# A hybrid attention/scan/FFN block on one core: first FFN column pair as eight plain products, and gate pieces of the dense filler moved to the end of the scan

## The chip, the cores and the metric

One Trainium2 chip, one core. The metric is the device time of one launch in microseconds (us); lower is better. The five engines are named as in the profile: PE (TensorE matmuls; PEld is its weight load), DVE (VectorE), ACT (ScalarE), POOL (GpSimd) and SP (SyncE, which here only issues DMAs).

## The reference, cut to what matters

One layer on 1024 tokens of width 1024, all in float32: a norm, one wide projection, three token mixers (two attentions of 8 heads and a state-space scan of 16 heads), a gated merge, then an FFN with a causal convolution.

```
u = rms_norm(x) @ w_in                       # split: mla | fox | ssm (z, xBC, dt) | gate (3 x 1024)
xBC = silu(causal_dwconv(xBC))               # 4 taps; input of the scan
y_a = mla(u_mla) @ w_br_mla;  y_b = fox(u_fox) @ w_br_fox;  y_c = ssd(u_ssm) @ w_br_ssm
g = sigmoid(u_gate + b_gate)
x = x + (g0 * y_a + g1 * y_b + g2 * y_c) @ w_out
a = causal_dwconv(rms_norm(x) @ w_up)        # w_up: 1024 x 5632; 3 taps
gate, val = split(a, 2)                      # 2816 columns each
x = x + (silu(gate) * val) @ w_down
```

## The kernel before, in words

Every large product is made of three float32r matmuls (high by high, high by low, low by high part). An operand is therefore "split": ACT copies it rounded into a high tile (line 142 in `split`), DVE subtracts to get the low tile (line 143). A matmul moves 512 columns through a 128x128 weight block.

**The dense filler.** 36 column blocks of 128 columns of `u` (12 of xBC, called conv blocks, and 24 gate blocks, `g_d`) are not computed in a stage of their own. The generator `all_fill` produces them in pieces of six matmuls (line 794, target `mm`); after each piece it yields 1.3 (us, the planner's price of a piece). A block has two halves of 24 matmuls, so 8 pieces; there are 288 pieces, 1728 matmuls. Before a block's matmuls its weights are loaded by SP (`wr`, 512 KB, line 741) and split on ACT and DVE (lines 744, 745). Behind each half ACT reads PSUM: a plain copy for conv blocks (line 799 and 801), a tanh for gate blocks. A conv block then runs its taps on POOL, DVE and ACT and is stored to `xbc_d`; a gate block is stored to `g_d` by SP (line 808). The list `blocks` sets the order of the blocks.

**Who pulls the filler.** `merge(streams, fill_us)` interleaves the streams of one step (for attention: scores of one unit, values of the unit two before; for the scan: parts a, b, c of chunks c, c-1, c-2) with `fill_us` worth of filler. In attention, 64 units plus two, it is `FILL_ATT` times the planner's cost of the unit's own PE work (which adds up to 231.7 over all units); in the scan's ten steps it is `FILL_SSD[c]`. Before attention 8.0 are taken, before the scan 10.0. Within attention and scan the PE order is the planner's; the other engines are placed by the scheduler. What is left of the filler after the scan is drained before the branch products start.

**End of the scan.** For the last chunk, part b ends with a multiplication by z (line 1153), a square with row sum on ACT (line 1156) into the single `yT` buffer, a reciprocal square root on DVE, and a scaling on ACT (line 1161); part c transposes the result on PE (`stp`, line 1169), ACT copies it to `yT` (line 1170) and SP stores it (`ys_d`, line 1172). Then the branch products follow (`ybr`, line 167 in `mm3`), in the order fox, mla, ssm. Each first loads its input (`ar`, through four buffers `t4` that the filler's gate tiles and z tiles also use), splits it (`ah`, `al`), and multiplies.

**The FFN's up projection.** It runs over 22 column pairs i (gate columns i and value columns i + 22). Rows are in two halves of 512 tokens, the contraction in two halves of 512 features; `B11`, `B21`, `T1`, `B22` are the four blocks or sums of the normed activations. A pair is computed by a Strassen-Winograd scheme in seven block products of 12 matmuls (`product`, line 1319) in place of eight: `ua` two (against B11 and B21), `ub`, `uc` twice, `ud` twice. The scheme needs sums of weights (`sums`, on POOL: S12 and S34, lines 1409 to 1413), which are then split, and sums of activations `T3`, `T2`, `T4`, made once: the buffer `T3f` is split into the high and low tiles `cbh` and `cbl` (`t_split`, lines 1442 and 1445), then changed in place (`t_sums`, lines 1452 to 1456, two of four rows on DVE, two on POOL), and split again. The `ua` products of the first four pairs are taken early, right behind the output projection `wo`, and kept in `cg`. Each pair ends with the convolution (lines 1515 to 1523) on ACT and DVE. The raw weights of a pair sit in two `wr` buffers, so the next pair's loads wait for this pair's sums and for the split of a third piece (`h22`).

All PE work from `wo` on stands in written order (`order2`).

Of the kernel before, what the change touches and what calls it, by code (L numbers as in the profile page):

```python
# [11 lines left out]
F32 = mybir.dt.float32  # L12
# [3 lines left out]
AF = mybir.ActivationFunctionType  # L16
ALU = mybir.AluOpType
# [4 lines left out]
P = 128  # L22
# [15 lines left out]
def f32(ap):  # L38
    return ap.bitcast(F32)
# [3 lines left out]
def block_kernel(ctx: ExitStack, tc: tile.TileContext, x, positions, norm_mix_g, w_in, b_gate,  # L43
# [91 lines left out]
    def uid(s):  # L135
        cnt[0] += 1
        return f"{s}_{cnt[0]}"
# [639 lines left out]
    def all_fill():  # L777

        conv = [("c", j, C_XBC + j * P) for j in range(12)]
        gates = [(b, j, C_G + b * D + j * P) for b in (1, 0, 2) for j in range(NK)]  # L780
        blocks = [e for n in range(12) for e in (conv[n], gates[n])] + gates[12:]
        nxt = fill_load(blocks[0][2])
        for n, (kind, j, c0) in enumerate(blocks):
            wh, wl, rl = nxt
            if n + 1 < len(blocks):
                nxt = fill_load(blocks[n + 1][2])
            force(rl[0])
            u, ul = f_t4.get()
            for half in range(2):
                ps, pl = f_ps.get()  # L790
                hs = slice(512 * half, 512 * half + 512)
                for k in range(NK):
                    for i, (a, b) in enumerate(((wh, hnh), (wh, hnl), (wl, hnh))):
                        T.matmul(ps, a[:, k, :], b[half][:, k, :], start=(k == 0 and i == 0),  # L794
                                 stop=(k == NK - 1 and i == 2))
                    if k % 2 == 1 and k < NK - 1:
                        yield 1.3
                if kind == "c":
                    fn = lambda ps=ps, hs=hs, u=u: A.activation(u[:, hs], ps, AF.Copy)
                else:  # L800
                    fn = lambda ps=ps, hs=hs, u=u, r=8 * kind + j: A.activation(
                        u[:, hs], ps, AF.Tanh, bias=pc_g[:, r:r + 1], scale=0.5)
                pl[0] = later(1.4, fn)
                if half == 1:
                    if kind == "c":
                        conv_done(j, u, ul, 2.2)
                    else:
                        ul[0] = later(2.0, lambda u=u, g=g_d[kind][j]: SY.dma_start(g, u))
                yield 1.3
# [172 lines left out]
    def cost_v(jp):  # L982
        return 0.88 * jp + 0.33 + 0.39

    FILL_ATT = 1.08
    FILL_SSD = [12.0] * 8 + [12.0, 8.0]
    with ExitStack() as pt__:
        atp = pt__.enter_context(TP("atp", 2))
        psp = pt__.enter_context(TP("psa", 1, space=PSUM))
# [332 lines left out]
    def bank(name):  # L1322
        return psp.tile([P, 512], F32, name=uid(name), tag="up", bufs=6)
# [28 lines left out]
    xrp = po_.enter_context(TP("x2p", 1))  # L1352
    gff = bcast(norm_ffn_g[0], D, "gff", xrp)
    x2r = [None] * NT
    first = []
    units = [(t, nh) for nh in range(2) for t in range(3)] + [(t, nh) for t in range(3, NT) for nh in range(2)]

    head = [psp.tile([P, 512], F32, name=uid("wo"), tag="up", bufs=6) for _ in range(3)]
# [9 lines left out]
    for t, nh in units:  # L1368
        ns = slice(512 * nh, 512 * nh + 512)
        if nh == 0 and 4 <= t < 4 + FIRST:  # L1370
            n = t - 4
            if n == 0:
                r0 = raws(pairs[0])
                raw = r0[0]
            else:
                raw = fpl.tile([P, NK, P], F32, name=uid("wr"), tag="t4", bufs=4)
                SY.dma_start(raw, upv[:, :, pairs[n] * P:pairs[n] * P + P])
            first.append(halves(raw) if n < 3 else raw)
# [18 lines left out]
    a_ = []  # L1397
    for n in range(3):
        a_.append(bank("ua"))
        product(a_[n], first[n], 0, *B11)  # L1400
    norm2(NT - 1, x2r[NT - 1])
    po_.close()

# [9 lines left out]
        G.tensor_sub(S34[:, 4:8, :], ri[:, 4:8, :], S12[:, 4:8, :])  # L1413
        return S12, S34

    S_ = sums(*r0)
    h22_ = halves(r0[1][:, 4:8, :], 4)
    done_ = []
    for n in range(3):
        c_ = upb.tile([P, S], F32, name=uid("cg"), tag="cg", bufs=FIRST)  # L1420
        A.activation(c_[:, 512:], a_[n], AF.Copy)
        done_.append(c_)
    for n in range(FIRST):
        if n == 3:
            first[n] = halves(first[n])
            a_.append(bank("ua"))
            product(a_[n], first[n], 0, *B11)
            done_.append(upb.tile([P, S], F32, name=uid("cg"), tag="cg", bufs=FIRST))
            A.activation(done_[n][:, 512:], a_[n], AF.Copy)
        product(a_[n], first[n], 4, *B21, first=False)  # L1430
        A.activation(done_[n][:, 0:512], a_[n], AF.Copy)
    cbp = pcb.enter_context(TP("cb", 1))
    cbh = cbp.tile([P, 12, 512], F32R, name="cbh", tag="cbh")
    cbl = cbp.tile([P, 12, 512], F32R, name="cbl", tag="cbl")
# [12 lines left out]
    def t_sums(second):  # L1447

        for k in range(4):
            e = G if k > 1 else V  # L1450
            if second:
                e.tensor_add(tf[k], tf[k], f32(B11[0][k]))
                e.tensor_add(tf[k], tf[k], f32(B11[1][k]))
            else:
                e.tensor_sub(tf[k], f32(B21[0][k]), tf[k])
                e.tensor_add(tf[k], tf[k], f32(B21[1][k]))

    def tmp(name, bufs=1):
        return upa.tile([P, 512], F32, name=uid(name), tag=name, bufs=bufs)

    for n, i in enumerate(pairs):
        early = n < FIRST
        ri, rj = r0 if n == 0 else raws(i)
# [9 lines left out]
        S12, S34 = S_ if n == 0 else sums(ri, rj)  # L1473
        hS12 = halves(S12)
        hS34 = halves(S34)
        h22 = h22_ if n == 0 else halves(rj[:, 4:8, :], 4)
        if n > 0:
# [7 lines left out]
        if n == 0:  # L1485
            t_split(T3)
        product(d0, hS34, 0, *T3)
        e5 = tmp("e5")
        A.activation(e5, c0_, AF.Copy)
        if n == 0:  # L1490
            t_sums(True)
            t_split(T2)
        e7 = tmp("e7")
        A.activation(e7, d0, AF.Copy)
        product(c0_, hS34, 4, *B22, first=False)
        if n == 0:
            t_sums(False)
            t_split(T4)
# [12 lines left out]
        V.tensor_add(cv[:, 0:512], d0, X)  # L1511
        av = []
        for j, c in ((i, cg), (i + NFF, cv)):
            a = fpl.tile([P, S], F32, name=uid("fa"), tag="t4", bufs=4)
            A.activation(a, c, AF.Identity, bias=pc_f2[:, 44 + j:45 + j], scale=pc_f2[:, j:j + 1])
            for d in (1, 2):
                w = pc_f1[:, 44 * (2 - d) + j:44 * (2 - d) + j + 1]
                V.scalar_tensor_tensor(out=a[:, d:], in0=c[:, :S - d], scalar=w, in1=a[:, d:],
                                       op0=ALU.mult, op1=ALU.add)
            av.append(a)  # L1520
        A.activation(av[0], av[0], AF.Silu)
        V.tensor_mul(av[1], av[0], av[1])
        SY.dma_start(act_d[i], av[1])

    wd = ffn_w_down[0].rearrange("(r p) c -> r p c", p=P)
# [150 lines left out]
```

## Time and profile before

| what | value |
|---|---|
| time, median of 3 runs | 2149.49 us (2144.91 to 2150.79) |
| time of the profiled execution | 2144.91 us |
| its span, first to last instruction | 2143.0 us |
| mean granted PE clock | 0.982 of full speed |
| busy: PE, DVE, ACT, POOL | 2042.3, 1402.9, 936.0, 649.0 us |
| filler matmuls (line 794) | 1728, in three groups of 576 |

The span is the time of the profiled execution less 1.9 us around it. That execution is the fastest of the three. Attention lies at about 436 to 973 us of the span, the scan at 973 to 1193, the branch products at 1207 to 1384, the output projection at 1384 to 1478, the up projection from 1478 to about 1935, and the down projection behind it.

### The profile page before, as it was taken

How to read it: one execution, taken by the hardware profiler on the slowest of the kernel's cores; microseconds unless marked ns; L12 is line 12 of the kernel's file. 1: busy time of each engine (PE TensorE's matmuls, PEld its weight loads, DVE VectorE, ACT ScalarE, POOL GpSimd, SP SyncE). 2: the span in 40 equal slices, each digit the busy share in tenths (PEclk: the TensorE clock that was granted, in tenths of full speed). 3: DMA queues.
4: the chain of work that ended last, by engine and by line, in shares of the span. 5: the costliest groups of instructions: out<-in, count | busy, mean ns of one | idle time of the engine just before them, and what ended most of it. 6: DMA issues, size and time to landing. Idle time of an engine off the chain costs nothing.

```text
span 2143.0 us, 29100 instructions
## 1 busy us (share of the span) xinstructions
PE 2042.3 (95%) x10253; PEld 1689.7 (79%) x10253; DVE 1402.9 (65%) x2590; ACT 936.0 (44%) x1677; POOL 649.0 (30%) x620
## 2 busy tenths in 40 slices
PE   7999898999999999999999799999889999999999
PEld 6898677778888787787777688888668888887887
DVE  6687477346666566665888446557976677665665
ACT  5554222145555555554555213223444454545432
POOL 2453132212222222220000021002655544441855
PEclk9999999999999999999999899999899999999999
DMA  5167668654343544524342556441122222229765
GB/s 169 33 190 222 220 216 240 205 156 126 96 137 97 138 121 109 131 86 127 105 134 89 162 184 204 140 134 61 49 86 82 88 79 80 88 74 338 260 217 190
DMA packets 276649, 303.61 MB, mean 142 GB/s; under 512 B 19308, under 2 KB 209784, under 8 KB 276504
## 3 DMA queue, kind: packets, MB, share of 16 engines
q1 hardware_dynamic: 276504, 301.76, 46.0%
q8 instruction: 81, 1.33, 0.3%
q14 instruction: 64, 0.52, 0.1%
HBM read 209.03 MB, written 92.67 MB: 141 GB/s over the span
## 4 chain that ended last, share of the span: by engine, by line
PE 78%; DVE 7%; DMA 5%; POOL 3%; ACT 3%; issue 3%; SPq 0%; DVEq 0%; ACTq 0%; POOLq 0%
PE mm L794 16%; PE dn L1626 10%; PE ybr L167 8%; PE ua L1319 5%; PE fx L167 5%; PE uc L1319 5%; PE ud L1319 4%; PE wo L1364 4%; PE s L884 3%; PE tp L952 2%; PE ub L1319 2%; PE fxv L167 1%; DMA raw<-in_w_in_dram 1%; PE kv L167 1%; PE q L167 1%
## 5 line engine op out<-in xcount | busy, mean ns | idle before, releaser
L794 PE MATMUL mm<-hnh,wh 128*128 128x512 f32 x576 | 248.6, 432 | 0.0
L906 POOL TENSOR_SCALAR pm<-pm,rs 128x128 f32<-128x128 f32 (+7 forms) x128 | 110.2, 864 | 402.6 <-DVE rs L905 242.1
L794 PE MATMUL mm<-hnh,wl 128*128 128x512 f32 x576 | 226.9, 394 | 0.0
L794 PE MATMUL mm<-hnl,wh 128*128 128x512 f32 x576 | 226.1, 393 | 0.0
L1626 PE MATMUL dn<-dr,dr 128*128 128x512 f32 x592 | 182.1, 389 | 0.0
L899 ACT ACTIVATE pm<-s,nmx 128x128 f32<-128x128 f32 (+2 forms) x192 | 110.2, 579 | 97.6 <-DVE nmx L896 70.2
L958 DVE TENSOR_TENSOR ptl<-tp,pth 128x512 fp32r<-128x512 f32 (+1 forms) x160 | 100.2, 633 | 70.3 <-ACT pth L957 68.7
L889 DVE TENSOR_REDUCE nmx<-s 128x1 f32<-128x128 f32 (+2 forms) x192 | 105.5, 553 | 56.6 <-PE s L887 44.6
L884 PE MATMUL s<-qk,qk 96*128 96x384 f32 (+5 forms) x480 | 120.8, 356 | 13.0 <-ACT pm L899 11.4
L957 ACT ACTIVATE pth<-tp 128x512 fp32r<-128x512 f32 (+1 forms) x160 | 88.1, 554 | 99.5 <-PE tp L952 99.0
L1626 PEld LDWEIGHTS dn<-dr,dr 128*128 128x128 f32 x592 | 111.1, 188 | 22.9
L794 PEld LDWEIGHTS mm<-hnh,wl 128*128 128x128 f32 x576 | 108.4, 188 | 25.1
L794 PEld LDWEIGHTS mm<-hnl,wh 128*128 128x128 f32 x576 | 109.2, 190 | 17.1 <-issue 2.9
L794 PEld LDWEIGHTS mm<-hnh,wh 128*128 128x128 f32 x576 | 109.5, 190 | 16.6 <-issue 2.9
L1235 POOL TENSOR_TENSOR mg<-mg,gl 128x512 f32<-128x512 f32 x16 | 24.9, 1561 | 311.4 <-DVE gl L1232 311.3
L1626 PE MATMUL dn<-dr 128*128 128x512 f32 x296 | 115.2, 389 | 0.0
L167 PE MATMUL fx<-w5h,hnh 128*128 128x512 f32 x256 | 101.9, 402 | 7.9 <-ACT w5h L142 7.9
L143 DVE TENSOR_TENSOR dr<-dr,dr 128x1024 fp32r<-128x1024 f32 x52 | 75.3, 1449 | 49.9 <-ACT dr L142 41.8
L142 ACT ACTIVATE wh<-wr 128x1024 fp32r<-128x1024 f32 (+1 forms) x46 | 42.0, 913 | 147.6 <-PE ybr L167 69.6
L884 PEld LDWEIGHTS s<-qk,qk 96*128 96x128 f32 (+1 forms) x480 | 81.3, 192 | 26.4 <-ACT pm L899 16.2
L167 PE MATMUL ybr<-ah,wh 128*128 128x512 f32 x256 | 100.2, 396 | 1.6 <-ACT ah L142 1.6
L167 PE MATMUL fx<-w5h,hnl 128*128 128x512 f32 x256 | 101.4, 397 | 0.0
(457 smaller groups left out, 5855.7 us busy)
## 6 DMA issues: line engine op xcount, KB each, us to landing
dr<-act_d SPq DMA_DIRECT2D x99, 256.0 KB
wr<-in_ffn_w_up_dram SPq DMA_DIRECT2D x47, 512.0 KB
wr<-in_w_in_dram SPq DMA_DIRECT2D x36, 512.0 KB
g_d<-t SPq DMA_DIRECT2D x24, 512.0 KB
gl<-g_d SPq DMA_DIRECT2D x24, 512.0 KB
ws<-in_ffn_w_down_dram SPq DMA_DIRECT2D x22, 512.0 KB
wsum_d<-ws SPq DMA_DIRECT2D x22, 512.0 KB
act_d<-fa SPq DMA_DIRECT2D x22, 512.0 KB
```

Source lines behind the costliest of these rows:

```text
L143: return i, le.tensor_sub(l, src, f32(h))
L167: T.matmul(ps, a(k), b(k), start=(i == 0), stop=(i == n - 1))
L794: T.matmul(ps, a[:, k, :], b[half][:, k, :], start=(k == 0 and i == 0), stop=(k == NK - 1 and i == 2))
L884: T.matmul(ps[:, :w], q_[:, qs], k_[:, a:a + w], start=i_ == 0, stop=not last and i_ == len(o.passes) - 1)
L889: later(c + 0.1, lambda ps=ps, ci=ci, a=a, b=b: V.reduce_max(nmx[:, ci:ci + 1], ps[:, :b - a], axis=AX, negate=True))
L899: pss[ci][1][0] = later(c + 0.9 + 0.1 * ci, lambda ci=ci, a=a, b=b: A.activation(p_[:, a:b], pss[ci][0][:, :b - a], AF.Exp, bias=nb, accum ...
L906: G.tensor_scalar(p_[:, 0:n * P], p_[:, 0:n * P], rs[:, 3:4], 0.0, op0=ALU.mult, op1=ALU.add)
L957: later(c + 0.05, lambda th=th, pt=pt, off=off: A.activation(th[:, :off], pt[:, :off], AF.Copy))
L958: pl[0] = later(c + 0.6, lambda th=th, tl=tl, pt=pt, off=off: V.tensor_sub(tl[:, :off], pt[:, :off], f32(th[:, :off])))
L1319: T.matmul(ps, a, b, start=first and n == 0, stop=n == 11, skip_group_check=not first)
L1364: T.matmul(p, a, b, start=k == 0 and i == 0, stop=k == NK - 1 and i == 2)
L1626: T.matmul(ps[m], a[:, ts_], b[:, 512:], start=first_ and j == 0 and q == 0, stop=j == NFH - 1 and q == 2, skip_group_check=not first_)
```

## The change

1. **Filler order and amounts.** The blocks stood conv, gate, conv, gate, ... until the conv blocks were out; now conv block n stands at place 20n // 11. `FILL_ATT` goes from 1.08 to 1.0, and the scan's amounts from eight steps of 12, then 12 and 8, to eight of 11, then 11 and 15.
2. **Pair 0.** It is computed by eight plain block products, without weight sums and without `T2` to `T4`. Its gate half uses `first[0]` against B11, B21 (as before), and T1, B22; its value half uses `hB`, the split of the raw value columns, against the same four. The early products are taken in the order of pairs 1, 2, 0, 3, and the eight plain ones, the early products of pair 3 and the making of T3 and T2 are interleaved by hand. T4 is made in pair 1, and the convolution of pair 0 (now the function `finish_pair`) runs there.
3. **`t_sums`.** All of its sums are on DVE.

```diff
-        blocks = [e for n in range(12) for e in (conv[n], gates[n])] + gates[12:]
+        blocks = list(gates)
+        for n in range(12):
+            blocks.insert(20 * n // 11, conv[n])
-    FILL_ATT = 1.08
-    FILL_SSD = [12.0] * 8 + [12.0, 8.0]
+    FILL_ATT = 1.0
+    FILL_SSD = [11.0] * 8 + [11.0, 15.0]
...
+    FORDER = (1, 2, 0, 3)
...
     def t_sums(second):
         for k in range(4):
-            e = G if k > 1 else V
             if second:
-                e.tensor_add(tf[k], tf[k], f32(B11[0][k]))
...
+                V.tensor_add(tf[k], tf[k], f32(B11[0][k]))
...
+    for n in FORDER[:3]:
+        keep_p1(n)
+    p2(1)
+    hB = halves(r0[1])
+    p2(2)
...
+    b0 = bank("ub")
+    product(b0, hB, 0, *B11)
+    f1 = tmp("e5")
+    A.activation(f1, b0, AF.Copy)
+    p2(0)
+    t_split(T3)
+    product(b0, hB, 4, *B21, first=False)
+    cv = fpl.tile([P, S], F32, name=uid("cv"), tag="t4", bufs=4)
+    A.activation(cv[:, 0:512], b0, AF.Copy)
+    t_sums(True)
+    c0_ = bank("uc")
+    product(c0_, first[0], 0, *T1)
+    first[3] = halves(first[3])
+    product(c0_, first[0], 4, *B22, first=False)
+    t_split(T2)
+    p1(3)
+    keep_p1(3)
+    d0 = bank("ud")
+    product(d0, hB, 0, *T1)
+    product(d0, hB, 4, *B22, first=False)
+    p2(3)
+    V.tensor_add(done_[0][:, 512:], c0_, done_[0][:, 512:])
+    V.tensor_add(cv[:, 512:], d0, f1)
+    plain = (pairs[0], done_[0], cv)
...
-    for n, i in enumerate(pairs):
+    for n, i in list(enumerate(pairs))[1:]:
...
+        if n == 1:
+            t_sums(False)
+            t_split(T4)
+        else:
             b0 = bank("ub")
             product(b0, hS12, 4, *T2)
...
+        if n == 1:
+            finish_pair(*plain)
```

(`p1(n)` and `p2(n)` are the early products of pair n's gate half against B11 and B21; `keep_p1` copies the first out of PSUM.) Below, rows of the built programs' instruction order. A name's number tells one buffer from another; "..." stands for rows left out.

PE at the end of the scan, before: `stp` with `y_12796` and `y_13041` are the last two transposes of chunks 6 and 7, and `ybr` is the first branch product.

```order
L1169 MATMUL stp_13316<-ident,y_12796 128x128 x4
...
L1134 MATMUL pof_13328<-hst_13175,bc_12733 128x512
L794 MATMUL mm_13280<-hnh_129,wh_12997 128x512
...
L1169 MATMUL stp_13361<-ident,y_12796 128x128 x4
L1169 MATMUL stp_13369<-ident,y_13041 128x128 x4
L1169 MATMUL stp_13376<-ident,y_13041 128x128 x4
L167 MATMUL ybr_13449<-ah_13419,wh_13443 128x512
```

PE at the same place now (chunk 6 is `y_12650`, chunk 7 `y_12889`); each `mm` number is one half block of 24 matmuls, of which the first row is shown.

```order
L1171 MATMUL stp_13215<-ident,y_12650 128x128 x4
L796 MATMUL mm_13150<-hnh_128,wh_12961 128x512
...
L796 MATMUL mm_13228<-hnh_129,wh_12961 128x512
...
L796 MATMUL mm_13259<-hnh_128,wh_13147 128x512
...
L1171 MATMUL stp_13308<-ident,y_12889 128x128 x4
...
L1171 MATMUL stp_13320<-ident,y_12889 128x128 x4
L796 MATMUL mm_13329<-hnh_128,wh_13256 128x512
...
L796 MATMUL mm_13385<-hnh_129,wh_13256 128x512
...
L167 MATMUL ybr_13449<-ah_13419,wh_13443 128x512
```

Before, no filler stood behind the second transposes of chunk 6; now 126 filler matmuls (21 pieces) stand between them and the first branch product: 72 ahead of chunk 7's transposes, 6 between these and 48 behind. Of the 21 pieces, 14 come from ahead of the scan's first transposes (1236 filler matmuls stood there, now 1152) and 7 from the scan.

PE in the first pair, before (first row of each product of 12; `ua` are early gate products, `uc_15633`, `ud_15646` and `ub_15715` belong to pair 0, `ub_15781` to pair 1).

```order
L1319 MATMUL ua_15468<-hnh_13413,wh_15246 128x512
...
L1319 MATMUL uc_15633<-hnh_13414,wh_15625 128x512
...
L1319 MATMUL ud_15646<-cbh,wh_15629 128x512
...
L1319 MATMUL ub_15715<-cbh,wh_15625 128x512
...
L1319 MATMUL ud_15646<-cbh,h_4615_15536 128x512
...
L1319 MATMUL ub_15781<-cbh,wh_15769 128x512
```

The same stretch now (`ub_15574` and `ud_15684` hold pair 0's value half, `uc_15632` its gate half, `uc_15762` and `ud_15775` belong to pair 1).

```order
L1321 MATMUL ub_15574<-hnh_13413,wh_15549 128x512
...
L1321 MATMUL uc_15632<-hnh_13414,wh_15246 128x512
...
L1321 MATMUL ua_15669<-hnh_13413,wh_15645 128x512
...
L1321 MATMUL ud_15684<-hnh_13414,wh_15549 128x512
...
L1321 MATMUL uc_15762<-hnh_13414,wh_15734 128x512
...
L1321 MATMUL ud_15775<-cbh,wh_15738 128x512
```

Before, pair 0's second product already read the T sums (`cbh`); now eleven products against plain blocks follow the last transposes of the norm, and the first reader of `cbh` is pair 1's second product.

DVE at the T sums, before (`T3f` rows of line 1455 and 1456 are sums, `cbl` rows the low part of a split).

```order
L1445 TENSOR_TENSOR cbl<-T3f,cbh 128x512 x2
L1455 TENSOR_TENSOR T3f<-hnh_13413,T3f 128x512
L1445 TENSOR_TENSOR cbl<-T3f,cbh 128x512
L1455 TENSOR_TENSOR T3f<-hnh_13413,T3f 128x512
L1445 TENSOR_TENSOR cbl<-T3f,cbh 128x512
L1456 TENSOR_TENSOR T3f<-T3f,hnl_13415 128x512 x2
```

DVE now, the piece of its list with pair 1's weight splits (`wl_15735` for S12, `wl_15739` for S34; `cg` and `cv` are pair 0's results, `fa` its convolution).

```order
L143 TENSOR_TENSOR wl_15735<-S_4629_15728,wh_15734 128x1024
L1459 TENSOR_TENSOR T3f<-T3f,hnl_13415 128x512
L1449 TENSOR_TENSOR cbl<-T3f,cbh 128x512
L1459 TENSOR_TENSOR T3f<-T3f,hnl_13415 128x512
L1471 SCALAR_TENSOR_TENSOR fa_15804<-cg_15534,pc_f_121,fa_15804 128x1023
L1449 TENSOR_TENSOR cbl<-T3f,cbh 128x512 x3
L1500 TENSOR_TENSOR cv_15622<-ud_15684,e_4619_15587 128x512
L1471 SCALAR_TENSOR_TENSOR fa_15804<-cg_15534,pc_f_121,fa_15804 128x1022
L143 TENSOR_TENSOR wl_15739<-S_4630_15731,wh_15738 128x1024
```

Between the first split of T3 and the split `wl_15739` DVE has 12 T splits, 16 sums and six other instructions; POOL has lost the T sums and pair 0's six instructions, and keeps the weight sums of pairs 1, 2 and so on.

More of the change, by code (lines that the diff above doesn't have):

```diff
@@ L1354, in block_kernel @@
     x2r = [None] * NT
-    first = []
+    first = {}
+    FORDER = (1, 2, 0, 3)
     units = [(t, nh) for nh in range(2) for t in range(3)] + [(t, nh) for t in range(3, NT) for nh in range(2)]
@@ L1370, in block_kernel @@
         if nh == 0 and 4 <= t < 4 + FIRST:
-            n = t - 4
+            n = FORDER[t - 4]
             if n == 0:
@@ L1377, in block_kernel @@
                 SY.dma_start(raw, upv[:, :, pairs[n] * P:pairs[n] * P + P])
-            first.append(halves(raw) if n < 3 else raw)
+            first[n] = halves(raw) if n < 3 else raw
         if nh == 0:
@@ L1396, in block_kernel, with p1 @@
     T1, B22 = [(rows(h2h[1], k), rows(h2l[1], k)) for k in (0, 4)]
-    a_ = []
-    for n in range(3):
-        a_.append(bank("ua"))
+    a_, done_ = {}, {}
+    def p1(n):
+        a_[n] = bank("ua")
         product(a_[n], first[n], 0, *B11)
+    for n in FORDER[:3]:
+        p1(n)
     norm2(NT - 1, x2r[NT - 1])
@@ L1414, in sums, with keep_p1, p2 @@
         return S12, S34
[L1416 to L1429, printed above, removed]
+    def keep_p1(n):
+        done_[n] = upb.tile([P, S], F32, name=uid("cg"), tag="cg", bufs=FIRST)
+        A.activation(done_[n][:, 512:], a_[n], AF.Copy)
+    def p2(n):
         product(a_[n], first[n], 4, *B21, first=False)
         A.activation(done_[n][:, 0:512], a_[n], AF.Copy)
+    for n in FORDER[:3]:
+        keep_p1(n)
+    p2(1)
+    hB = halves(r0[1])
+    p2(2)
     cbp = pcb.enter_context(TP("cb", 1))
@@ L1449, in t_sums, with finish_pair @@
         for k in range(4):
-            e = G if k > 1 else V
             if second:
-                e.tensor_add(tf[k], tf[k], f32(B11[0][k]))
-                e.tensor_add(tf[k], tf[k], f32(B11[1][k]))
-            else:
-                e.tensor_sub(tf[k], f32(B21[0][k]), tf[k])
-                e.tensor_add(tf[k], tf[k], f32(B21[1][k]))
+                V.tensor_add(tf[k], tf[k], f32(B11[0][k]))
+                V.tensor_add(tf[k], tf[k], f32(B11[1][k]))
+            else:
+                V.tensor_sub(tf[k], f32(B21[0][k]), tf[k])
+                V.tensor_add(tf[k], tf[k], f32(B21[1][k]))
     def tmp(name, bufs=1):
         return upa.tile([P, 512], F32, name=uid(name), tag=name, bufs=bufs)
-    for n, i in enumerate(pairs):
+    def finish_pair(i, cg, cv):
+        av = []
+        for j, c in ((i, cg), (i + NFF, cv)):
+            a = fpl.tile([P, S], F32, name=uid("fa"), tag="t4", bufs=4)
+            A.activation(a, c, AF.Identity, bias=pc_f2[:, 44 + j:45 + j], scale=pc_f2[:, j:j + 1])
+            for d in (1, 2):
+                w = pc_f1[:, 44 * (2 - d) + j:44 * (2 - d) + j + 1]
+                V.scalar_tensor_tensor(out=a[:, d:], in0=c[:, :S - d], scalar=w, in1=a[:, d:],
+                                       op0=ALU.mult, op1=ALU.add)
+            av.append(a)
+        A.activation(av[0], av[0], AF.Silu)
+        V.tensor_mul(av[1], av[0], av[1])
+        SY.dma_start(act_d[i], av[1])
+    b0 = bank("ub")
[23 more added lines that the diff above has]
+    for n, i in list(enumerate(pairs))[1:]:
         early = n < FIRST
-        ri, rj = r0 if n == 0 else raws(i)
+        ri, rj = raws(i)
         if early:
@@ L1472, in block_kernel @@
         e1 = cg[:, 512:]
-        S12, S34 = S_ if n == 0 else sums(ri, rj)
+        S12, S34 = sums(ri, rj)
         hS12 = halves(S12)
         hS34 = halves(S34)
-        h22 = h22_ if n == 0 else halves(rj[:, 4:8, :], 4)
-        if n > 0:
+        h22 = halves(rj[:, 4:8, :], 4)
+        if n == 1:
+            t_sums(False)
+            t_split(T4)
+        else:
             b0 = bank("ub")
@@ L1484, in block_kernel @@
         d0 = bank("ud")
-        if n == 0:
-            t_split(T3)
         product(d0, hS34, 0, *T3)
@@ L1489, in block_kernel @@
         A.activation(e5, c0_, AF.Copy)
-        if n == 0:
-            t_sums(True)
-            t_split(T2)
         e7 = tmp("e7")
@@ L1495, in block_kernel @@
         product(c0_, hS34, 4, *B22, first=False)
-        if n == 0:
-            t_sums(False)
-            t_split(T4)
+        if n == 1:
+            finish_pair(*plain)
             b0 = bank("ub")
@@ L1511, in block_kernel @@
         V.tensor_add(cv[:, 0:512], d0, X)
[L1512 to L1523, printed above, removed]
+        finish_pair(i, cg, cv)
     wd = ffn_w_down[0].rearrange("(r p) c -> r p c", p=P)
```

## The prediction

> **What bounds the kernel now.** I read the page first, then busy time by stage, then the idle of PE in the two places that the change touches, then the chain of waits there.
>
> ```profile
> PE 2042.3 (95%) x10253; PEld 1689.7 (79%) x10253; DVE 1402.9 (65%) x2590; ACT 936.0 (44%) x1677; POOL 649.0 (30%) x620
> 436.00:973.00 537.00, 515.57 (x3026) 429.48 (x3027) 342.88 (x790) 288.00 (x702) 130.98 (x143) 0.99 0.43 116
> 973.00:1193.00 220.00, 219.89 (x1096) 165.79 (x1095) 170.03 (x327) 106.79 (x174) 0.00 (x0) 1.00 0.39 116
> 1193.00:1214.00 21.00, 9.01 (x29) 7.01 (x28) 8.20 (x17) 8.72 (x12) 0.00 (x0) 0.59 0.61 189
> 1480.00:1545.00 65.00, 56.06 (x222) 42.10 (x221) 56.22 (x59) 30.49 (x45) 34.06 (x20) 0.89 0.16 52
> 1545.00:1600.00 55.00, 46.96 (x188) 36.83 (x188) 39.41 (x34) 22.11 (x27) 31.90 (x19) 0.94 0.27 87
> 1600.00:1930.00 330.00, 330.00 (x1456) 272.83 (x1455) 230.02 (x209) 161.44 (x190) 156.88 (x98) 1.00 0.25 82
> ```
>
> PE is the bound: busy 95% of the span, without a gap in the scan (219.9 of 220) and in the later pairs (330 of 330). So PE work that only moves is worth nothing; what can be won is idle or slow-clock time of PE. It lies at the scan's end (9.0 busy of 21, granted clock 0.59), in the first pairs (clock 0.89 and 0.94, 17 us idle in two stretches) and in attention (21 us idle of 537). The change adds 12 matmuls and no other PE work.
>
> **Scan's end: filler moved in.** PE's rows and the chain there:
>
> ```profile
> 1192.79 0.60 PE L1169 MATMUL stp<-ident,y 128*128 128x128 f32 x4
> 1203.74 1.97 PE L1169 MATMUL stp<-ident,y 128*128 128x128 f32 x8 [10.36 <-ACT y L1161]
> 1207.35 2.08 PE L167 MATMUL ybr<-ah,wh 128*128 128x512 f32 x4 [1.63 <-ACT ah L142]
> 1213.42 0.39 PE L167 MATMUL ybr<-ah,wl 128*128 128x512 f32 x1
> 1194.47 4.82 DMA ys_d<-yT
> 1199.39 1.16 ACT yT L1156 x2
> 1202.54 1.16 ACT y L1161
> 1182.96 2.76 PE mm L794 x12
> 1605.60 2.72 PE ub L1319 x12
> ```
>
> Twelve dense matmuls take 2.72 us at full clock, 0.227 each; a piece of six 1.37. After chunk 6's last transposes PE waits 10.36 us, because chunk 7's square may not write `yT` until chunk 6's store has left it (4.82 us), then 1.63 more; and the first 14 branch matmuls take 6.07 us (1207.35 to 1213.42) instead of 3.2. From 1193.3 to 1213.4 PE had 3.2 us of matmuls and 0.9 of transposes (estimate: half of their cold 1.97) to do: 16.0 us are lost.
>
> Now 126 filler matmuls, 21 pieces, 28.6 us, stand in that place: 72 (16.3 us) ahead of chunk 7's transposes, which the chain above lets start 10.9 us after chunk 6's (1192.79 to 1203.74). So the transposes no longer wait, and the gap of 1.63 is filled as well. What must ride along: the pieces' weight loads, their splits on ACT and DVE, the tanh reads and the stores of three gate blocks. One weight split stands on ACT behind the square and on DVE behind the square root, but it serves the last block only, whose matmuls start 17 us later. On SP the four `ar` loads now stand behind chunk 7's store, which waits for the second copy to `yT`, some 19.7 us after the start of this stretch; then 10.9 us of filler are left. Three 512 KB loads behind a store at about the 4.8 us of the row above, shared, land within about 10 us; the fourth waits for the first's split, 6 to 7 us later than its load, and is needed 35 matmuls (8 us) into the branch. It has about 4 us of slack, so I cost it at nothing; without it, up to 4.8 us, one transfer. Saved at most 16.0.
>
> The pieces leave holes where they were: 14 ahead of the scan (19.2 us of PE work), 7 in the scan (9.6 us).
>
> ```profile
> PE s L884 <- ACT pm L899: 11.4, 6, 3.1
> PE o L924 <- ACT o L937: 5.3, 9, 1.1
> PE o L924 <- DVE o L940: 3.1, 7, 0.8
> 1125.00:1150.00 25.00, 25.00 (x128) 18.90 (x127) 21.24 (x42) 12.97 (x22) 0.00 (x0) 1.00 0.25 76
> ```
>
> PE's waits in attention are 22 in 66 steps. A removed piece that stood at such a place costs its whole 1.37, elsewhere nothing: 14 x 22/66 x 1.37 = 6.4 us at most by this count. I take 3, since these waits last 0.9 us on the mean, less than a piece; the ends are 0 (a little below, if the pieces' own ACT and DVE work made some of the waits) and 19.2. At attention's end 27 filler matmuls stood between the last values and the scan's first transposes, and none do now: 1 us, ends 0 and 6. In the scan PE waits for nothing and DVE is busy 21.2 of 25 us per chunk; a chunk with one piece less has 23.6, still above DVE's 21: 1 us, ends 0 and 9.6. Sum for this part: -16 + 3 + 1 + 1 = **-11 us**, ends -16 and +19.
>
> **Up projection: plain pair 0.** Rows of PE, first of each stretch:
>
> ```profile
> 1477.80 0.48 PE L1319 MATMUL ua<-hnh,wh 128*128 128x512 f32 x1
> 1487.70 0.47 PE L1319 MATMUL ua<-hnh,wh 128*128 128x512 f32 x1
> 1526.62 0.79 PE L1319 MATMUL ud<-cbl,h 128*128 128x512 f32 x1 [1.99 <-DVE cbl L1445]
> 1570.21 0.50 PE L1319 MATMUL uc<-hnh,wh 128*128 128x512 f32 x1 [2.08 <-ACT e L1489]
> 1574.21 0.63 PE L1319 MATMUL ud<-cbh,h 128*128 128x512 f32 x1
> 1574.64 0.63 PE L1319 MATMUL ud<-cbl,h 128*128 128x512 f32 x1
> 1577.40 0.39 PE L1319 MATMUL ua<-hnh,wh 128*128 128x512 f32 x1
> 1595.54 0.75 PE L1319 MATMUL uc<-hnh,wh 128*128 128x512 f32 x1 [2.82 <-ACT e L1489]
> 1602.72 0.39 PE L1319 MATMUL ua<-hnh,wh 128*128 128x512 f32 x1
> ```
>
> 1477.80 is the first early product, 1577.40 the start of pair 4, 1602.72 of pair 5. Between the first and the last lie 124.9 us for 35 products (95.2 us) and 0.8 of transposes: **28.9 us lost**, half of it on the low parts of the T sums, the rest on weight sums and on the slow clock (two products from 1570.21 take 7.19 instead of 5.44). Now there are 36 products. Why the T sums were late:
>
> ```profile
> 1495.00:1529.00 34.00, 25.71 (x89) 17.21 (x88) 33.97 (x28) 13.41 (x21) 24.11 (x14) 0.83 0.05 15
> 1495.54 2.38 DVE L1445 TENSOR_TENSOR cbl<-T3f,cbh 128x512 fp32r<-128x512 f32 x2
> 1500.14 0.68 DVE L1452 TENSOR_TENSOR T3f<-T3f,hnh 128x512 f32<-128x512 f32 x1
> 1500.30 1.68 POOL L1452 TENSOR_TENSOR T3f<-T3f,hnh 128x512 f32<-128x512 f32 x1 [1.23 <-DVE cbl L1445]
> 1500.75 1.78 DVE L1445 TENSOR_TENSOR cbl<-T3f,cbh 128x512 fp32r<-128x512 f32 x1
> 1526.49 1.27 DVE L1518 SCALAR_TENSOR_TENSOR fa<-cg,pc_f,fa 128x1023 f32<-128x1023 f32 x1
> 1548.79 3.63 DMA wr<-in_ffn_w_up_dram
> 1534.89 1.28 POOL L1409 TENSOR_TENSOR S<-wr 128x512 f32<-128x512 f32 x1 [10.01 <-DMA wr<-in_ffn_w_up_dram]
> 1552.55 1.67 POOL L1409 TENSOR_TENSOR S<-wr 128x512 f32<-128x512 f32 x1 [6.07 <-DMA wr<-in_ffn_w_up_dram]
> 1558.83 1.23 DVE L143 TENSOR_TENSOR wl<-S,wh 128x1024 fp32r<-128x1024 f32 x1 [3.52 <-ACT wh L142]
> 1569.90 1.55 POOL L1409 TENSOR_TENSOR S<-wr 128x512 f32<-128x512 f32 x1 [7.45 <-DMA wr<-in_ffn_w_up_dram]
> ```
>
> DVE is full there (33.97 of 34), but its instructions are stretched: a sum of 512 elements takes 0.68 us (0.61 from start to start), and 1.78 when it meets one of POOL's. POOL's alone takes 1.28. From 1495.5 to 1528.4 DVE had 22 such instructions, three weight splits (1.15 from start to start) and one of 1.2: 18.1 us if alone; POOL had 14, 17.9 us. Together 36.0, and 32.8 us went by: the two hardly overlap, 0.91 of the sum. The Trainium skill, SBUF — State Buffer, section "SBUF: two separate sides", says that a DVE instruction with two SBUF inputs and one of GpSimd exclude each other for their whole length. By that the factor below would be 1 and the sum of this part 2.8 us worse; the trace, at 0.91, nearly agrees, and I go by it.
>
> The new schedule, in the same clock. Eleven plain products from 1487.70, whose operands need no sums, end at 1517.6; pair 1's first ends at 1520.3, and the third matmul of its second (about 1520.8) needs the low part of S34. DVE reaches that split after 12 T splits, 16 sums, three more of 512 (31 x 0.61 = 18.9), two of 1.2 and two weight splits (2.3): 23.6 us, with six POOL sums (7.7) in between, 0.91 x 31.3 = 28.5, so at 1524.0. A wait of 3.2 us; with POOL free beside it none, with eight POOL sums in full 8.6. The clock then falls: 1.8 us, as after 1570.21. Pair 1 ends at 1536.2. Its T2 and T4, and the moved convolution of pair 0, stand on DVE ahead of or behind this and are done 5 us before PE asks.
>
> From there the weights set the pace. After the last split of a raw block: load 3.63, sums, splits; 1548.79 to 1560.06, 11.3 us. Pair 2's were summed during the plain products. Pair 3's block is freed at about 1540.7, its weights are ready at 1552; PE asks at 1550.4: 1.5. Pair 4's likewise 1.2. Pair 5's sum holds up ACT ahead of a read that PE needs (as at 1595.54): 2.6, and 1.8 of clock. So pair 5 starts at 1536.2 + 27.2 + 1.5 + 19.0 + 1.2 + 2.6 + 1.8 = 1589.5, 13.2 us earlier; 2 us I take off, because the weights are then 12 us ahead of PE and were 14.6. **-11 us**. Ends: 36 products without a wait, -26; all 28.9 lost again, +2.7.
>
> The Trainium skill, TensorE: Matmul & The Clock Gate, section "Part 1: The HAM clock gate", has the clock fall only after an idle window of about 3.4 us. Here a wait of 2.08 was followed by matmuls 0.43 apart (1574.21 to 1574.64), so the two clock terms stay; by the page this part would be up to 3.6 us better.
>
> **Sum.** 2144.9 (the profiled execution: span 2143.0 and 1.9 around it) - 11 - 11 = 2122.9. That execution is 4.6 below the median of the runs; taking half of this, **2125 us**. About 0.3%, 6 us, is what a measurement here can tell from no change.
>
> **Rivals.**
> - *Attention needs its cover.* All 14 pieces leave their 19.2 us behind as waits: -16 + 21 - 11 = -6, 2139 to 2143. For it: attention already has 21 us of waits. Against: they are 22 short ones, and ACT (288 of 537) and DVE (343) are far from full. 0.14.
> - *The weights' chain stays the pace of the pairs.* S sums started 17.5 us apart (1534.89 to 1569.90 over two pairs), PE needs 13.6: if pairs 2 to 4 keep that, 11 us of waits in place of 2.7, the gain falls to 3, and 2131 to 2135 comes out. 0.12.
> - *Neither place gains*: -6 to 0, 2139 to 2149. 0.07.
> - *Slower: the clock stays low through pairs 1 to 3.* At 0.43 per matmul a product costs 2.4 us more; 15 products 36 us, 2159. It needs a wait every two or three microseconds, as DVE's splits gave from 1512 to 1529. It decides from about 12 cold products (28 us against 22 gained). Against: T2 and T4 are ready before they are asked for. 0.07.
>
> The forecast itself holds 0.60, with 2110 to 2134. Range 2110 to 2142: it takes in the second rival and most of the first. Faster 0.83 (forecast, second, most of the first), same 0.10, slower 0.07.
>
> **What would show it.** Right: no wait of PE over 2 us between the last transposes of chunk 6 and the first branch products, granted clock 1.0 there; attention with under 25 us of waits; pair 0's products back to back; one wait at pair 1's second product; about 13 us fewer from the first early product to pair 5. Wrong: waits on `s` or `o` in attention grown by 10 us and more, `ar` loads late at the first branch product, or pairs 2 to 4 each waiting for POOL's sums.

## The result, and the profile after

The changed kernel takes 2123.3 us (median of four runs, 2119.9 to 2128.0), the kernel before 2149.1 beside it: a ratio of 0.9891, 95% interval 0.9874 to 0.9907, or 20 to 27 us less. 2125 was forecast. The profiled execution took 2120.2 (span 2118.1), which is 3.1 below the median; the profiled one of before lay 4.6 below its median, so the two traces may be compared stage by stage. One stage calls for care: attention's length differs by up to 7 us between profiles of the same instructions (last section).

The page's row of busy times, and busy time by stage (columns: start and end, length, busy time of PE, weight loads, DVE, ACT, POOL with counts, granted clock, DMA share, GB/s):

```profile
PE 2036.5 (96%) x10250; PEld 1688.7 (80%) x10265; DVE 1395.2 (66%) x2595; ACT 935.3 (44%) x1675; POOL 626.2 (30%) x606
422.26:960.66 538.40, 517.82 (x3041) 431.88 (x3039) 345.33 (x791) 289.32 (x703) 131.58 (x143) 0.99 0.44 119
962.70:1166.97 204.27, 200.33 (x975) 149.21 (x991) 165.84 (x322) 101.27 (x165) 0.00 (x0) 0.98 0.39 114
1166.97:1196.95 29.98, 29.98 (x139) 24.88 (x138) 5.84 (x15) 10.30 (x15) 0.00 (x0) 1.00 0.44 140
1464.62:1508.00 43.38, 42.60 (x193) 34.82 (x190) 37.99 (x56) 22.81 (x36) 11.72 (x6) 1.00 0.16 49
1508.00:1520.00 12.00, 8.58 (x27) 6.88 (x28) 11.03 (x8) 5.14 (x6) 5.74 (x3) 0.72 0.15 44
1520.00:1576.49 56.49, 52.33 (x224) 41.41 (x224) 43.72 (x38) 26.79 (x31) 31.81 (x19) 1.00 0.28 93
```

The rows are attention, the scan, the scan's end, and three pieces of the first pairs. Taken between the same events (first filler to last values, the scan's first transposes to chunk 6's last, first early product to pair 5), the kernel before has for attention, the scan and the first pairs:

```profile
426.34:978.89 552.55, 530.26 (x3099) 441.44 (x3098) 345.57 (x793) 291.33 (x707) 130.98 (x143) 0.99 0.44 117
984.90:1192.79 207.89, 207.78 (x1034) 155.63 (x1033) 165.40 (x317) 103.38 (x169) 0.00 (x0) 1.00 0.39 115
1477.80:1602.72 124.92, 107.95 (x431) 83.00 (x430) 99.84 (x97) 55.62 (x74) 66.72 (x39) 0.92 0.21 68
```

The scan's end is full now (29.98 of 29.98 at clock 1.00; before, 9.0 of 21 at 0.59). The first pair is nearly full; one piece, 1508 to 1520, has a wait and a low clock. And the scan, where PE had no gap before, has 3.9 us of idle and a clock of 0.98. (At a granted clock of 1.00 matmuls of 512 columns start 0.227 us apart, in a slow stretch 0.43.) PE's waits that answer to this:

```profile
962.70 0.66 PE L1078 MATMUL stp<-ident,t 128*128 128x128 f32 x4 [2.05 <-DVE o L942]
1067.80 0.66 PE L1171 MATMUL stp<-ident,y 128*128 128x128 f32 x4 [2.10 <-ACT y L1163]
1511.42 0.79 PE L1321 MATMUL ud<-cbh,wl 128*128 128x512 f32 x1 [4.20 <-DVE wl L143]
1562.01 0.50 PE L1321 MATMUL ua<-hnh,wh 128*128 128x512 f32 x1 [2.57 <-ACT cg L1513]
1576.49 0.39 PE L1321 MATMUL ua<-hnh,wh 128*128 128x512 f32 x1
```

The first row is the end of attention. The second is the transposes of the scan's chunk 2 (chunks counted from 0, as in chunk 6 and 7 above), which fall in the step of chunk 4; an expectation below calls it the fourth chunk. The third is pair 1's second product, the fourth lies in pair 4, and the last is the start of pair 5. In the new order the first `ua` row stands at 1464.62 and the first `ybr` at 1196.95.

### The profile page after: what moved, and what is told of

Read it like the earlier page. It is cut to its first block, busy times and chain, and to the rows that moved or that the text cites. A ratio compares the mean times of both kernels' runs of the same rounds, so it can differ in the third digit from the quotient of the medians.

```text
span 2118.1 us, 29113 instructions
## 1 busy us (share of the span) xinstructions
PE 2036.5 (96%) x10250; PEld 1688.7 (80%) x10265; DVE 1395.2 (66%) x2595; ACT 935.3 (44%) x1675; POOL 626.2 (30%) x606
## 4 chain that ended last, share of the span: by engine, by line
PE 76%; DMA 8%; DVE 8%; ACT 2%; issue 2%; POOL 2%; SPq 1%; DVEq 0%; ACTq 0%; POOLq 0%
PE mm L796 15%; PE dn L1652 10%; PE ybr L167 8%; PE ua L1321 5%; PE uc L1321 4%; PE ud L1321 4%; PE wo L1367 4%; PE fx L167 4%; PE s L886 4%; PE tp L954 2%; DMA att_d<-o 2%; PE ub L1321 2%; PE fxv L167 1%; PE cq L167 1%; PE kv L167 1%
## 5 line engine op out<-in xcount | busy, mean ns | idle before, releaser
L908 POOL TENSOR_SCALAR pm<-pm,rs 128x512 f32<-128x512 f32 (+7 forms) x128 | 106.7, 837 | 383.2 <-DVE rs L907 256.8
L796 PEld LDWEIGHTS mm<-hnl,wh 128*128 128x128 f32 x576 | 110.1, 191 | 18.8 <-issue 3.9
L167 PE MATMUL fx<-w5l,hnh 128*128 128x512 f32 x256 | 101.3, 397 | 0.0
```

The source lines that it names most:

```text
L167: T.matmul(ps, a(k), b(k), start=(i == 0), stop=(i == n - 1))
L908: G.tensor_scalar(p_[:, 0:n * P], p_[:, 0:n * P], rs[:, 3:4], 0.0, op0=ALU.mult, op1=ALU.add)
```

## The experiments

Times in microseconds; each kernel ran several times beside the kernel before on one chip, and the ratio is to that.

**The filler alone.** The kernel before with the new block places and amounts.

```diff
-        blocks = [e for n in range(12) for e in (conv[n], gates[n])] + gates[12:]
+        blocks = list(gates)
+        for n in range(12):
+            blocks.insert(20 * n // 11, conv[n])
-    FILL_ATT = 1.08
-    FILL_SSD = [12.0] * 8 + [12.0, 8.0]
+    FILL_ATT = 1.0
+    FILL_SSD = [11.0] * 8 + [11.0, 15.0]
```

> The kernel before with only the dense pieces moved (block places, FILL_ATT 1.0, FILL_SSD 11 and 15 at the end); the first pair stays as before. By the two traces, stage against stage: scan's end -15.9, the scan itself +5.9 (one wait of 2.1 in the fourth chunk and slow-clock matmuls behind two waits), attention -1.2, its end +2.1: about -9 us, 2140. By the prediction's terms -11, 2138. Rival: the 4.1 us by which the changed kernel reached attention earlier belong to the change too, then -13, 2136. Rival: the store of yT is late in this kernel too and part of the saving at the end goes, then -5 or less.

Measured: 2137.1 against 2142.7, ratio 0.9966 (0.9950 to 0.9982): 4 to 11 us less. The point is 7; the rival of -13 is out. The interval alone does not exclude the rival of -5 or less, but the trace does: from chunk 6's last transposes to the first `ua` it takes 297.5 us, as in the changed kernel (297.65). PE's waits in this kernel, in attention, the scan and the scan's end:

```profile
PE s L886 <- ACT pm L901: 11.1, 4, 3.1
PE o L926 <- DVE o L942: 2.4, 1, 2.4
PE stp L1171 <- ACT y L1163: 2.1, 1, 2.1
PE stp L1078 <- DVE o L942: 2.0, 1, 2.0
```

The two `stp` waits are those of the changed kernel, and no wait of 10 is left. The block places and the amounts were not run apart, so what each is worth stays open.

**The plain first pair alone.** The changed kernel with the old block places and amounts (the lines above, the other way).

> The changed kernel with the dense pieces where they were before: only the plain first pair is new. By the two traces -13.0 from the first early product to pair 5 and +1.3 behind it: about -12 us, 2137. If the two parts add up, this and the filler alone give -21 to -26 together. Rival: the first pair gained in part because the filler shifted the loads ahead of it; then it is worth less alone, 2142 or more, and the two don't add up.

Measured: 2133.5, ratio 0.9953 (0.9935 to 0.9971): 6 to 14 us less. From the first early product to the down projection it took 437.5, as the changed kernel (437.3), where the kernel before has 449.0. The loads ahead of the pair, then, did not make the gain. By the runs the two parts are 7 and 10, 17 in all, where the whole change has 23 and 21 to 26 were expected: less, but within the intervals (4 to 11 and 6 to 14), so that the parts may add and need not. PE's long waits behind attention in this kernel are those of before at the scan's end and the changed kernel's in the pairs:

```profile
PE stp L1169 <- ACT y L1161: 10.3, 1, 10.3
PE ud L1319 <- DVE wl L143: 4.2, 1, 4.2
PE ua L1319 <- ACT cg L1511: 2.6, 1, 2.6
PE ybr L167 <- ACT ah L142: 1.6, 1, 1.6
```

**What the 10.36 us waited for.** The kernel before, with one operand changed:

```diff
-            A.activation(o.yT.rearrange("p j s -> p (j s)"), yf, AF.Square, accum_out=ss)
+            A.activation(zt, yf, AF.Square, accum_out=ss)
```

> The kernel before; the square's unwanted elementwise output goes to the spent gate tile zt instead of yT, so that it no longer waits for the store of the chunk before. If that store is what made PE wait 10.36 us at the scan's end, the square starts at 1194.3 instead of 1199.4, the wait falls to about 5.2 and the kernel gains 5 us: 2144. Rival: the y chain on DVE and ACT sets the wait whatever the store does; the wait stays at 9 to 10 and the time at 2149.

Measured: 2136.7, ratio 0.9973 (0.9958 to 0.9988), 3 to 9 us less. ACT and PE at the scan's end (`t` is the tile of `zt`):

```profile
1197.38 0.59 ACT L1170 ACTIVATE yT<-stp 128x512 f32<-128x512 f32 x1
1197.85 1.06 ACT L1156 ACTIVATE t<-y 128x1024 f32<-128x1024 f32 x1
1202.21 1.97 PE L1169 MATMUL stp<-ident,y 128*128 128x128 f32 x8 [5.30 <-ACT y L1161]
1205.81 1.65 PE L167 MATMUL ybr<-ah,wh 128*128 128x512 f32 x3 [1.63 <-ACT ah L142]
```

The square follows the copy at once, and PE's wait falls from 10.36 to 5.30. Half of what the filler covers was a wait for a store: the square threw an output that nobody reads into a buffer that was still being stored. The other half is the chain of the norm. The store is shown as the cause of that half.

**T sums on two engines again.** The changed kernel with this:

```diff
         for k in range(4):
+            e = G if k > 1 else V
             if second:
-                V.tensor_add(tf[k], tf[k], f32(B11[0][k]))
+                e.tensor_add(tf[k], tf[k], f32(B11[0][k]))
...
```

> The changed kernel with half of the T sums back on POOL (k of 2 and 3). If DVE and POOL hardly overlap on two-input instructions (0.91 of the sum went by in the trace of before), DVE loses 8 sums of 0.61 (4.9 us) and POOL gains 8 of 1.28 (10.2 us): the low part of S34 comes 0.91 x 5.3 = 4.8 us later, PE's wait of 4.2 grows to about 9, and the kernel is 5 us slower: 2128. Rival: the two engines work side by side; then the low part comes up to 4.9 us earlier, the wait of 4.2 and the slow clock behind it go: 4 to 6 us faster, 2118. Third: the sums are not on the path of that wait, no change.

Measured: 2126.5, ratio 0.9925 (0.9903 to 0.9948), where the changed kernel has 0.9891 and, in a second set, 0.9881: slower by some 7 us, though the intervals overlap at their ends. In the trace the stretch from the first early product to the down projection takes 440.6, where the two profiles of the changed kernel have 437.3 and 436.0 and the kernel before 449.0. So in the stage that the edit touches it costs 3 to 5 us, and the plain products keep 8 us of their gain even with the sums on two engines. DVE, POOL and PE there:

```profile
1504.32 3.48 DVE L1449 TENSOR_TENSOR cbl<-T3f,cbh 128x512 fp32r<-128x512 f32 x2
1503.81 3.44 POOL L1457 TENSOR_TENSOR T3f<-T3f,hnl 128x512 f32<-128x512 f32 x2
1516.01 0.51 PE L1321 MATMUL ua<-hnh,wh 128*128 128x512 f32 x1 [4.00 <-ACT cg L1425]
1525.45 0.50 PE L1321 MATMUL ud<-cbh,wh 128*128 128x512 f32 x1 [2.07 <-ACT wh L142]
```

Two low parts of DVE (from 1504.32) take 3.48 beside two sums of POOL (from 1503.81) in 3.44; in the changed kernel, with POOL idle, DVE's take 0.68 each and start 0.60 apart. So the four need some 3.5 us together; one after the other, at 0.60 and at the 1.28 of POOL's row alone, they would need 3.8. The direction was as expected, the place was not: PE waits 4.00 for a bank whose copy stands on ACT behind a split that waits for POOL, then 2.07 and 0.52 for S34. The rival that the engines work side by side is out.

**Fewer pieces at the scan's end.** Of the 21 pieces 11 stay; with the square's output in `zt`.

```diff
-    FILL_ATT = 1.0
-    FILL_SSD = [11.0] * 8 + [11.0, 15.0]
+    FILL_ATT = 1.01
+    FILL_SSD = [11.7] * 8 + [11.7, 9.0]
-            merge([], 10.0)
+            merge([], 14.0)
```

> The changed kernel with the square's unwanted output in zt (as in the run of the kernel before with that edit) and 10 of the 21 pieces put back: 5 ahead of the scan, 5 in it, 11 left at its end (48 matmuls ahead of the last transposes, 10.9 us against the 5.9 that they need; 18 behind, 4.1 us against 1.6). If the cost of the moved pieces is what the traces show (2.1 at attention's end, 5.9 in the scan, by a wait of 2 us and the slow clock behind it in each), both go and the time falls by 6 to 8 us against the changed kernel: 0.9965 of it. Rival: PE is full in the scan, a piece put back costs what it saves at the end, 0 to -2. Rival: with less filler the ar loads come late at the first branch products, +2 to +5.

Measured: 2120.7, ratio to before 0.9882 (0.9861 to 0.9903), beside 0.9881 of the changed kernel: no difference that the runs can show. In the trace both `stp` waits are gone, but a new one stands at the first branch product:

```profile
1192.85 2.94 ACT L142 ACTIVATE ah<-ar 128x1024 fp32r<-128x1024 f32 x3
1193.95 1.20 PE L167 MATMUL ybr<-ah,wh 128*128 128x512 f32 x4 [2.01 <-ACT ah L142]
```

Attention's first filler to the first branch product takes 769.5, against 774.7 and 772.3 in the two profiles of the changed kernel, the new wait of 2 included. But attention, with its scatter, is part of that. From its last values on it takes 233.4 (231.8 in the kernel with both edits below), and the five profiles with the new filler and without this edit have 233.0 to 236.3. So a gain of a few us is possible and not shown, and the rival (a piece put back costs what it saves, 0 to -2) stands. Since `zt` and the pieces were changed at once, which of them took the scan's wait away is open too. The new wait is not for a late load (three loads were there when ACT began) but for ACT's order: a weight split and a tanh read come first. The 6 to 8 us were too much.

**T4 later.** The changed kernel with the T4 sums behind pair 1's third product.

```diff
         if n == 1:
-            t_sums(False)
-            t_split(T4)
-        else:
+        if n > 1:
...
         product(c0_, hS34, 4, *B22, first=False)
         if n == 1:
+            t_sums(False)
+            t_split(T4)
             finish_pair(*plain)
```

> The changed kernel with the sums and the split of T4 written behind pair 1's third product. On DVE four low parts of T4 leave the place ahead of the low part of S34, which comes 3.6 us earlier by their rows (0.68 and 2.98). If that split is what PE waits 4.2 us for, the wait falls to about 0.6 and the clock stays up: -4 to -6 us. Rival: T4's low parts, now last on DVE, come 1 to 3 us late for pair 1's product against T4 at 1521.6, and no more than 2 us are left of the gain.

Measured: 2120.4, ratio 0.9885 (0.9866 to 0.9903), again no difference to be told from the changed kernel. The wait at pair 1's second product falls to

```profile
1508.76 0.50 PE L1321 MATMUL ud<-cbh,wl 128*128 128x512 f32 x1 [1.70 <-DVE wl L143]
```

and the matmuls behind it run at full clock. But a new wait follows at the next product, for a copy that stands on ACT behind pair 0's convolution:

```profile
1512.51 0.50 PE L1321 MATMUL uc<-hnh,wh 128*128 128x512 f32 x1 [1.18 <-ACT e L1529]
```

The stretch up to the down projection takes 435.3 (434.9 with both edits), and 436.0 to 437.5 in four profiles with T4 in its old place. The sign is right; the size is about 2, not 4 to 6. That is the rival's size, but not its reason: PE does not wait for T4's low parts.

**Both, and the changed kernel once more.**

> Both edits of the two runs beside it. They lie 300 us apart, so their gains add: -10 to -14 against the changed kernel, 0.994 of it and 0.983 of the kernel before. Rival: what one gains the other's stage gives back through the clock or the loads, and the sum is under 5.

> The changed kernel once more, as the measure of the three beside it and for a second profile of the same code: 0.989 of the kernel before. Its waits in attention should be those of the first profile to 0.1 us; if the runs differ by 5 us and more all the same, it is the clock behind those waits: more matmuls 0.43 apart where the time is longer.

Measured: both edits 2114.9, ratio 0.9866 (0.9844 to 0.9888); the changed kernel beside it 2117.6, 0.9881 (0.9855 to 0.9906). By the two stretches named, 771.0 and 434.9, the kernel with both edits is 1 to 4 and 1 to 2 us ahead of the changed kernel; by the medians it is 2.7. That is the rival's sum (under 5), not the 10 to 14 expected, and for the first stretch it is within attention's scatter. The second profile of the changed kernel has the same long waits of `s` to 0.03, but one of `o` is 2.37 where it was 3.27, so they are not all the same to 0.1. The kernel with both edits has the lowest median of all, and these runs do not separate it from the changed kernel.

## Why the prediction was right

**The scan's end: -16 forecast, -15.9 measured.** From chunk 6's last transposes (1192.79 before, 1166.97 after) to the first `ua` (1477.80, 1464.62) lie 285.0 and 297.65 us, 12.6 more with 28.6 us of filler added. The trace with `zt` shows the store as half of the cause.

**About 4 us of slack for the fourth `ar` load: about 3 found.** Its high part is ready at 1202.06; 35 matmuls into the branch, where the prediction has its first use, PE is at 1205.00. The thin place is another: the first high part is ready at 1196.08, under 1 us ahead of its use, so there the cover was nearly used up.

```profile
1195.02 1.06 ACT L142 ACTIVATE ah<-ar 128x1024 fp32r<-128x1024 f32 x1 [2.61 <-DMA ar<-att_d]
1201.00 1.06 ACT L142 ACTIVATE ah<-ar 128x1024 fp32r<-128x1024 f32 x1 [1.40 <-DMA ar<-att_d]
1196.95 0.62 PE L167 MATMUL ybr<-ah,wh 128*128 128x512 f32 x2
```

**Attention: 3 forecast, about 0 measured.** From the first filler to the last values the three profiles with the old filler took 552.6, 555.4 and 555.4, five with the new 538.4 to 545.2, mean 541.4: 13.1 less, with 57 matmuls (12.9) fewer. So within the scatter the pieces filled no wait worth its time, and the rival that attention needs its cover (19 us) falls: PE is idle there for 20.6 us, and was for 22.3. The waits of `s` are as before; one wait of `o`, 3.3 here, is new, and the many short ones have become fewer:

```profile
PE s L886 <- ACT pm L901: 11.9, 5, 3.2
PE o L926 <- DVE o L942: 4.4, 4, 3.3
PE o L926 <- ACT o L939: 2.0, 5, 0.7
```

**Attention's end: 1 forecast, 2.1 measured** (the wait of 2.05, 6.01 us of filler gone).

**The scan: 1 forecast, 5.9 measured in the first profile; this is the term that was mis-sized.** From the scan's first transposes to chunk 6's last it took 207.89 before and 204.27 now, with 9.6 us of filler fewer. The step "a chunk with one piece less has 23.6, still above DVE's 21" counted engines by their sums. What gave way is one chain: y's square, again behind the store of `yT` (it ends at 1053.7), the norm's small instructions on DVE, scattered among others until 1065.2, then `y` behind a weight split on ACT. In chunk 2 it came 2.1 us late, and the slow clock behind this wait and the one at attention's end, with gaps under 0.3 us, cost the rest. The chain is read from the trace; no run took one link of it away alone. The second profile shows how much of the 5.9 is clock: it has the same waits (2.0 and 2.0) at a granted clock of 1.00, and 2.6 us in all. The mean over the five profiles with the new filler is 4.7.

So the filler part is about -9 by the traces and -7 (4 to 11) by the runs; -11 was forecast.

**The first pairs: -13.2 worked out, -13.05 measured, -11 taken.** From the first early product to pair 5 there were 124.92 us, now 111.87. Pair 0 runs back to back. The one wait at pair 1's second product is there: forecast for 1524.0 in the clock of before, it ends at 1511.4, which is 1524.6 counted from the first early product; 4.2 us instead of 3.2. The slow clock behind it cost more than the 1.8 taken: from 1506.61 to 1518.91 two products took 12.3 us, of which 5.4 are their work and 4.2 the wait, so 2.7 (1.9 in the second profile). Pair 1 was over 1.3 us later than worked out. Pairs 2 and 3 took 27.9 us where 28.7 were worked out, pair 4 took 24.3 (waits of 2.6 and three of 0.5, no slow clock) where it was 24.6. The 2 us taken off for the weights were not needed. The rival in which their chain paces the pairs shows in part: POOL's sums start 17.1 and 18.8 us apart,

```profile
1531.26 1.50 POOL L1416 TENSOR_TENSOR S<-wr 128x512 f32<-128x512 f32 x1 [7.31 <-DMA wr<-in_ffn_w_up_dram]
1548.37 1.65 POOL L1416 TENSOR_TENSOR S<-wr 128x512 f32<-128x512 f32 x1 [7.36 <-DMA wr<-in_ffn_w_up_dram]
1567.12 1.41 POOL L1416 TENSOR_TENSOR S<-wr 128x512 f32<-128x512 f32 x1 [6.92 <-DMA wr<-in_ffn_w_up_dram]
```

but PE entered pair 2 with sums made during the plain products, and only pair 4, with its seven products, feels it. From pair 5 to the down projection it takes 325.4 where it was 324.0, by one wait of 1.3. The slower rival (a low clock through pairs 1 to 3) did not come: 1.00 from 1520 on. Its condition was read too narrowly, though: before, the waits that went with a clock of 0.65 from 1512 to 1529 stood 2.3 to 5.3 us apart (1515.06, 1517.34, 1521.30, 1526.62), not two or three.

**The sum.** -9.1 and -11.7 by the two traces against -11 and -11. The mechanisms named are there, but that the sum comes out within 2 us is in part luck: the errors are small and of opposite sign, with three terms of the filler part that were 3, 1 and 1 and are -1, 2 and 6 there (0, 2 and 5 over all profiles). The remaining 4.1 us between the two profiled executions lie ahead of attention (first filler at 426.34 and 422.26), where nothing was changed; in the ten profiles that point lies anywhere from 420 to 427.

## What to carry to other kernels

Filler work is worth the idle and slow time of PE that it covers (here 28.6 us of it saved the 16 that were lost at the scan's end), and nothing where PE is full; but a stage that is full on the sum of its work may still have one chain with a slack of a piece or two, and that chain, not the sum, says what a piece taken away costs. A buffer used as a bin for an unwanted output ties an instruction to that buffer's store: look for a dead tile to write to. Splitting two-input sums between DVE and POOL gained nothing here: it cost 3 to 5 us in its stage against leaving them all on DVE.

## What the runs showed of the hardware that was not expected

**The same wait slows the clock in one execution and not in the next.** In pair 4 PE waits 2.57 us in the changed kernel and 2.56 in the one with T4 later. First the one, then the other:

```profile
1562.01 0.50 PE L1321 MATMUL ua<-hnh,wh 128*128 128x512 f32 x1 [2.57 <-ACT cg L1513]
1562.35 0.40 PE L1321 MATMUL ua<-hnl,wh 128*128 128x512 f32 x1
1562.58 0.39 PE L1321 MATMUL ua<-hnh,wl 128*128 128x512 f32 x1
```

```profile
1559.52 0.50 PE L1321 MATMUL ua<-hnh,wh 128*128 128x512 f32 x1 [2.56 <-ACT cg L1513]
...
1560.92 0.63 PE L1321 MATMUL ua<-hnh,wl 128*128 128x512 f32 x1
1561.34 0.63 PE L1321 MATMUL ua<-hnh,wh 128*128 128x512 f32 x1
1561.77 0.63 PE L1321 MATMUL ua<-hnl,wh 128*128 128x512 f32 x1
...
1563.90 0.46 PE L1321 MATMUL uc<-hnh,wh 128*128 128x512 f32 x1
```

There the slow stretch begins 1.4 us after the wait has ended, matmuls start 0.43 apart, and it is over after some 3 us. The two profiles of the changed kernel show the same with identical instructions. Attention's third long wait of `s` lasts 2.47 in the first and 2.44 in the second, its fourth 3.16 and 3.12. The 5 us from the end of each wait, first profile, then second (the last three columns are the granted clock, DMA share, GB/s):

```profile
776.75:781.75 5.00, 5.00 (x27) 4.00 (x27) 5.00 (x13) 3.93 (x11) 1.57 (x1) 1.00 0.39 118
866.00:871.00 5.00, 4.30 (x24) 3.22 (x25) 4.83 (x12) 3.27 (x9) 0.96 (x2) 1.00 0.25 98
```

```profile
776.31:781.31 5.00, 5.00 (x20) 4.15 (x21) 4.35 (x10) 3.27 (x10) 0.93 (x1) 0.66 0.39 111
866.26:871.26 5.00, 5.00 (x15) 3.91 (x16) 4.10 (x11) 3.16 (x9) 0.80 (x1) 0.50 0.24 97
```

This is where attention's scatter comes from. In the five profiles with the new filler it takes 538.4, 539.3, 541.1, 542.8 and 545.2 us, and in the same order PE is busy 517.8, 521.6, 523.4, 525.0 and 526.6 us with the same 3041 matmuls, of which 8, 17, 20, 23 and 28 of the filler are slow ones (0.61 to 0.63 us long instead of 0.39). The Trainium skill, TensorE: Matmul & The Clock Gate, section "Part 1: The HAM clock gate", says that the activity window of about 3.4 us runs freely and does not start with the work. That agrees with the late start and the chance in it; its rule that a whole idle window is needed does not agree with waits of 2.0 to 2.6 us that slowed the clock here. So the prediction's two clock terms of the pairs, 1.8 each, are a price that is paid in some executions only: the wait of 4.2 paid 2.7 (a clock of 0.72 from 1508 to 1520), the one of 2.57 in pair 4 paid nothing in this execution and some 1.3 to 1.7 us in four of the other six with these pairs.
